# A separate 16-bit copy of the rows for the third pass of two projections

## The chip, the cores and the metric

One NeuronCore of a Trainium2 chip. The metric is the device time of one execution in microseconds (us); lower is better. All inputs, weights and the output are 32-bit floats in device memory.

## What is computed

One block of a decoder for 512 rows (tokens) of 2048 columns. The stages, in the reference's words cut to what matters:

```python
h = rms_norm(x, norm1_g[l])
z = h @ w_in[l]
...
o_rw = rwkv7_mix(...)            # 512 x 1024
o_att = swa_attention(...)       # 512 x 1024
p_rw = o_rw @ w_branch[l, :RW_DIM]
p_att = o_att @ w_branch[l, RW_DIM:]
x = x + (g_rw * p_rw + g_att * p_att) @ w_out[l]
...
u = h @ w_up                     # 2048 x 11264, h = rms_norm(x, norm2_g[l])
c = up[:, 0:S] * conv_w[0] + up[:, 1:S + 1] * conv_w[1] + up[:, 2:S + 2] * conv_w[2] + conv_b
val, gate = jnp.split(c, 2, axis=-1)
x = x + (silu(gate) * val) @ w_down
```

The change concerns two of the five projections: the branch projection (`w_branch`) and the up projection (`w_up`).

## The kernel before, in words

**Precision.** TensorE multiplies in a rounded 32-bit type (`F32R`) or in 16 bits (`BF16`). Every projection splits both operands into a high part in `F32R` and a low part in `BF16`: ScalarE (ACT) copies the 32-bit number into the high part, which rounds it, and VectorE (DVE) subtracts the high part from the number to get the low part. Each weight block of 128 x 128 is then multiplied in three passes which add into the same accumulator in PSUM:

1. high weights by high rows, both `F32R`;
2. the upper 16 bits of the high weights by low rows;
3. low weights by the upper 16 bits of the high rows.

The upper 16 bits are not stored apart. The helper `top` (lines 247 to 249) reads the high part as pairs of 16-bit numbers and takes every second one, so the operand's numbers lie four bytes apart. The weights are the stationary operand of a matmul, loaded first; the rows are the moving operand.

**Order of the stages.** Input projection with attention and the recurrence in between (up to about 1124 us of the profile), branch projection (1124 to 1298), output projection (to 1454), up projection (to 2316), down projection (to the end).

**Branch projection** (lines 980 to 1001). There are 16 strips of 128 output columns, and for each two parts: the recurrent rows `rhi`, `rlo` and the attention rows `ahi`, `alo`, eight blocks of 128 in each. `project` (line 273) goes through a part in groups of four weight blocks: `load_w` (line 255) loads 256 KB on the SyncE queue, splits it (ACT at L262, DVE at L263) into one of four buffers, and then the three passes follow, four matmuls of 512 columns each (L283). The rows are split ahead of the stage by `split` (L216, L217): the recurrent rows pinned in program order, two at a time with a gate's strip of the input projection between them, the attention rows left to the scheduler.

**Up projection** (class `Block`, lines 1150 on). Matrix multiplication in seven products instead of eight per column block, on halves of rows and columns. Rows are held as seven operands of 8 blocks x 256 columns, named `b11`, `b21`, `b22`, `t1`, `t2`, `t3`, `t4`; each has a high and a low tile in `bq`. There are 44 column blocks with seven products each, named `P1`, `P2`, `P7`, `P6`, `P5`, `Q4`, `P3`. A product takes one weight tile of 128 x 1024: `prep` splits it two steps ahead (ACT at L1177, DVE at L1179, three buffers), `run` issues its 24 matmuls of 256 columns (three passes of eight, L1196). The instructions of this stage are pinned to program order on each engine.

The row operands are made while the first products already run: `high` (L1142) is an ACT copy of 2048 columns, `low` (L1146) the DVE subtract. Between them stand DVE sums that make one operand from others (L1388, L1393, L1403, L1414), and the weight splits of `prep`. The calls are written out by hand; a cutting of it:

```python
prep(9)
pin(dve.scalar_tensor_tensor(q12, q11, -1.0, q22, op0=ALU.mult, op1=ALU.subtract))   # L1403
run(7)
...
high("t2", q12)
prep(10)
run(8)
low("t2", q12)
```

`run(8)` to `run(11)` are the products `P7` of the first four column blocks and use `t3`; `run(12)` is the first that uses `t2`.

**Memory.** Tiles are taken from pools that are stacked from the left or the right end of the memory; a tile that comes to lie on an earlier one waits for that one's last use. The two result tiles `u0`, `u1` of the up projection are cleared at their edge by GpSimd (POOL) at L1424.

Of the kernel before, what the change touches and what calls it, by code (L numbers as in the profile page):

```python
# [9 lines left out]
F32R = mybir.dt.float32r  # L10
F16 = mybir.dt.float16
BF16 = mybir.dt.bfloat16
I32 = mybir.dt.int32
AF = mybir.ActivationFunctionType
# [5 lines left out]
P = 128  # L20
S = 512
# [114 lines left out]
def block_kernel(ctx: ExitStack, tc: tile.TileContext, d: Dims, a: dict, out: bass.AP):  # L136
    nc = tc.nc
    act, dve, pool, pe, sync = nc.scalar, nc.vector, nc.gpsimd, nc.tensor, nc.sync
    NK, NP, NQ, NKV, NF = d.NK, d.NP, d.NQ, d.NKV, d.NF
# [29 lines left out]
    big1 = abc.enter_context(tc.tile_pool(name="big1", bufs=1))  # L169
# [40 lines left out]
    pin = tc.keep_in_program_order  # L210
# [4 lines left out]
    def split(hi, lo, src, pin=free):  # L215
        pin(act.activation(hi, src, AF.Copy))  # L216
        pin(dve.tensor_tensor(lo, src, hi.bitcast(F32) if hi.dtype == F32R else hi, op=ALU.subtract))  # L217
# [6 lines left out]
    for f in range(NPRE):  # L224
        w, t = a["w_up"][f], {n: up_d[f, n] for n in ("s3", "s1", "P6", "P3")}
# [21 lines left out]
    def top(x):  # L247
        x = x.bitcast(BF16)
        return x[(slice(None),) * (len(x.shape) - 1) + (slice(1, None, 2),)]
# [20 lines left out]
            sums_along()()  # L270
        return hi, lo

    def project(acc, src, xhi, xlo, pre=()):
        nk = src.shape[1]
        for k0 in range(0, nk, 4):
            n = min(4, nk - k0)
            whi, wlo = pre[k0 // 4] if k0 // 4 < len(pre) else load_w(src[:, k0 : k0 + n])
            ops = [[(whi[:, j], xhi[:, k0 + j]) for j in range(n)],
                   [(top(whi[:, j]), xlo[:, k0 + j]) for j in range(n)],
                   [(wlo[:, j], top(xhi[:, k0 + j])) for j in range(n)]]  # L280
            for i, part in enumerate(ops):
                for j, (l, r) in enumerate(part):
                    stream.append(pe.matmul(acc, l, r, start=k0 + i + j == 0, stop=k0 + n == nk and i == 2 and j == n - 1))  # L283
# [3 lines left out]
    def big(pl, nm, tag, dt=F32R):  # L287
        return pl.tile([P, BIG], dt, name=nm, tag=tag)

    def by_k(t, n=NK):  # L290
        return t[:, : n * S].rearrange("p (k s) -> p k s", s=S)
# [3 lines left out]
    if True:  # L295
        xhi = by_k(big(big1, "xhi", "h1"))
        xlo = by_k(big(big1, "xlo", "l1", BF16))
# [34 lines left out]

        def ztile(c0):
            acc = accp.tile([P, S], F32, name="acc", tag="acc")
            project(acc, zt[c0], xhi, xlo, first.pop(c0, ()))
            return acc

        acc_k = ztile(d.c_ka)
# [561 lines left out]
        xbs = ExitStack()  # L900
        xbp = xbs.enter_context(tc.tile_pool(name="xb", bufs=1, reuse_waits="tile"))
        tb = xbs.enter_context(tc.tile_pool(name="tb", bufs=4, reuse_waits="tile"))
        rhi, rlo = (xbp.tile([P, NP, S], t, name=f"r{e}") for e, t in (("hi", F32R), ("lo", BF16)))
        with tc.tile_pool(name="ain", bufs=1, side="right", reuse_waits="tile") as ainp:
            ain = [ainp.tile([P, NQ // 2, S], F32, name=f"ain{i}") for i in range(2)]
            rin = [ainp.tile([P, S], F32, name=f"rin{i}") for i in range(NP)]
            for i in range(NP):
                pool.dma_start(rin[i], o_rw_d[i])
            for i in range(2):
                pool.dma_start(ain[i], o_at_d.rearrange("(i n p) s -> i p n s", i=2, p=P)[i])  # L910
            wp["step"] = 4
            for i in range(4):
                emit_gate()

            for i in range(NP):
                split(rhi[:, i], rlo[:, i], rin[i], pin)
                if i % 2:
                    emit_gate()
            while gates:
                emit_gate()  # L920
            for ins, at in zip(entries, LAST):
                behind(ins, stream[base + at - 1])
            ahi = by_k(big(big1, "ahi", "h1"), NQ)
            alo = by_k(big(big1, "alo", "l1", BF16), NQ)
            for i in range(NQ):
                split(ahi[:, i], alo[:, i], ain[2 * i // NQ][:, i % (NQ // 2)])
    pa.close()


# [42 lines left out]
    with ExitStack() as pbb:  # L972
        accp = pbb.enter_context(tc.tile_pool(name="accB", bufs=4, space=PSUM, side="right", reuse_waits="tile"))
        mp = pbb.enter_context(tc.tile_pool(name="mt", bufs=2, side="right", reuse_waits="tile"))
        XC = NT * d.D // NK

        parts = ((rhi, rlo, 0, NP, 0), (ahi, alo, NP, NQ, 1))
        order = [(m + e, i) for m in range(0, NK - 4, 2) for i in (0, 1) for e in range(2)]
        order += [(m, i) for i in (1, 0) for m in range(NK - 4, NK)]
        g = {}  # L980
        for m, i in order:
            hi, lo, r0, n, gi = parts[i]
            second = m in g
            if not second:
                g[m] = tb.tile([P, 2, S], F32, name="gin", tag="gin")
                for j in range(2):
                    src = gate_d[(j * NK + m) * P : (j * NK + m + 1) * P]
                    if m < 4:
                        pin(sync.dma_start(g[m][:, j], src))
                    else:  # L990
                        act.dma_start(g[m][:, j], src)
            acc = accp.tile([P, S], F32, name="acc", tag="acc")
            project(acc, a["w_b"][m].rearrange("p (k c) -> p k c", c=P)[:, r0 : r0 + n], hi, lo)
            if second:
                w = min(XC, d.D)
                for e in range(m * XC, (m + 1) * XC, w):
                    t, c0 = divmod(e, d.D)
                    with tc.issue_after(wp["last"].ins):
                        sync.dma_start(x1(t, slice(c0, c0 + w)), xd[t * P : (t + 1) * P, c0 : c0 + w])
            gt = g[m][:, gi]  # L1000
            dve.scalar_tensor_tensor(gt, gt, 1.0, acc, op0=ALU.add, op1=ALU.mult)
            if second:

                dve.tensor_tensor(g[m][:, 0], g[m][:, 0], g[m][:, 1], op=ALU.add)
                if m % 2:
                    mt = [g[m + e][:, 0] for e in (-1, 0)]
                    tq = mp.tile([P, 4, TH], F32, name="tq", tag="tq")
                    factors(tq, *mt, 0)
                    factors(tq, *mt, 1)
                    store_factors(pool, "o", m // 2, *mt, tq)  # L1010
# [68 lines left out]

    upx = ExitStack()  # L1080
    bqp = upx.enter_context(tc.tile_pool(name="bqA", bufs=1, reuse_waits="tile"))
    bq = {n: [bqp.tile([P, KH, TH], t, name=f"{n}{i}") for i, t in enumerate((F32R, BF16))] for n in ("b11", "b21")}
    hp = hps.enter_context(tc.tile_pool(name="hhlO", bufs=3, reuse_waits="tile"))
    NCC = d.D // S
    ssp = tcp.tile([P, NT, NCC], F32, name="ssp")
# [52 lines left out]
    def halves(t):  # L1138
        return t.rearrange("p (a k) s -> p a (k s)", a=2)

    def high(n, q, pin=pin):
        pin(act.activation(halves(bq[n][0]), q, AF.Copy))  # L1142

    def low(n, q, pin=pin):
        hi, lo = (halves(x) for x in bq[n])
        pin(dve.tensor_tensor(lo, q, hi.bitcast(F32), op=ALU.subtract))  # L1146

    us = []
# [2 lines left out]
    class Block:  # L1151
# [29 lines left out]
        def mm(self, n):  # L1181
            if n == "P1":
                x = ups.tile([P, S], F32, name="X", tag="X")
                self.X = x[:, :TH]
                self.Z = x[:, TH:] if self.f < NPRE else upy.tile([P, S], F32, name="Z", tag="Y")[:, :TH]
            if n == "P7":
                self.Y = upy.tile([P, S], F32, name="Y", tag="Y")[:, :TH]
            into = {"P2": "Z", "P7": "Y", "Q4": "Y"}.get(n, "X")
            ps = getattr(self, "Z" if self.apart and n in ("P5", "P3") else into)
            start = n in ("P1", "P7") or n == "P2" and self.f >= NPRE or n == "P5" and self.apart  # L1190
            whi, wlo = (x.rearrange("p (k c) -> p k c", c=P) for x in self.hl.pop(n))
            xh, xl = bq[{"P1": "b11", "P2": "b21", "P7": "t3", "P6": "t2", "P5": "t1", "Q4": "t4", "P3": "b22"}[n]]
            for i in range(3):
                for k in range(KH):
                    l, r = ((whi[:, k], xh[:, k]), (top(whi[:, k]), xl[:, k]), (wlo[:, k], top(xh[:, k])))[i]
                    pin(pe.matmul(ps, l, r, start=start and k + i == 0, stop=k == KH - 1 and i == 2, skip_group_check=True))  # L1196

        def out(self, n):
# [141 lines left out]
    with tc.tile_pool(name="sqp", bufs=1, side="right", reuse_waits="tile") as sqp:  # L1340
# [3 lines left out]
        for i in range(len(PRODUCTS)):  # L1344
# [14 lines left out]
            if last:  # L1359
# [8 lines left out]


    bqp = upx.enter_context(tc.tile_pool(name="bqB", bufs=1, reuse_waits="tile"))  # L1370
    bq.update({n: [bqp.tile([P, KH, TH], t, name=f"{n}{i}") for i, t in enumerate((F32R, BF16))]
               for n in ("b22", "t1", "t3", "t2", "t4")})
    up = upx.enter_context(tc.tile_pool(name="upw", bufs=1, side="left", reuse_waits="tile"))

# [182 lines left out]
```

## Time and profile before

| | |
|---|---|
| median of 3 runs | 2743.89 us (2741.99 to 2744.76) |
| the profiled execution | 2743.16 us |
| its span, first to last instruction | 2741.3 us |
| granted TensorE clock, mean | 0.999 |
| branch projection, L283, matmuls of 512 columns | 1124 to 1298 us |
| up projection, L1196, matmuls of 256 columns | 1454 to 2316 us |

How to read the lines below. PE is TensorE's matmuls, PEld its weight loads, DVE VectorE, ACT ScalarE, POOL GpSimd, SP SyncE. A row of a group names line, engine, operation, output and inputs by the program's names (buffer numbers left out), the shape and the count; behind the bar stand the busy time of the group in us, the mean duration of one in ns, and the idle time before them with what ended it. A row of the timeline gives the start, the duration of the run of equal instructions, and in brackets the idle time before. Matmuls are pipelined: one lasts longer than the distance to the start of the next, and the busy time of a group counts overlapping time once. A few matmul records are missing from the trace. A row of waits gives who waited for whom, the time in all, how often, and the longest.

### The profile page before, as it was taken

What the parts mean: (1) busy time and instruction counts of PE and PEld (TensorE: products, weight loads), DVE (VectorE), ACT (ScalarE), POOL (GpSimd) and SP (SyncE); (2) the same over time, 40 slices, a digit from 0 to 9 for tenths busy, and PEclk for the clock granted to TensorE, in tenths of its full rate; (3) what the DMA queues carried; (4) which work ended last, traced back from release to release, by engine and by line L of the source; (5) the groups of instructions that cost most, each with busy time, mean ns of one, the idle gap of its engine ahead of it and who ended that gap; (6) DMA issues with size and microseconds to landing.
All of it is one profiled execution on the core that took longest, in us unless ns stands there. A gap on an engine that the chain in (4) does not pass through costs nothing.

```text
span 2741.3 us, 45720 instructions
## 1 busy us (share of the span) xinstructions
PE 2685.9 (98%) x17227; PEld 1832.6 (67%) x17410; DVE 1995.1 (73%) x3476; ACT 1334.9 (49%) x2245; POOL 231.3 (8%) x308
## 2 busy tenths in 40 slices
PE   8999999999999999999999999999999999999999
PEld 4555566566566665555558889999999998555554
DVE  6787777777887775445668788888888888555655
ACT  5455445534544543322466555555555555444443
POOL 0001011111111001011000111111111110000000
PEclk9999999999999999999999999999999999999999
DMA  6557788778878767888785889898898889877775
GB/s 237 156 152 203 203 215 217 207 193 228 213 186 221 187 180 188 269 249 283 253 281 166 229 238 250 250 241 235 243 251 244 236 239 278 299 241 245 258 257 180
DMA packets 228333, 623.80 MB, mean 228 GB/s; under 512 B 24960, under 2 KB 45072, under 8 KB 227088
## 3 DMA queue, kind: packets, MB, share of 16 engines
q1 hardware_dynamic: 159552, 445.23, 49.3%
q0 software_dynamic: 37216, 136.33, 25.7%
q10 hardware_dynamic: 31344, 39.31, 4.1%
q8 instruction: 136, 2.23, 0.3%
q14 instruction: 85, 0.70, 0.1%
HBM read 571.16 MB, written 191.18 MB: 278 GB/s over the span
## 4 chain that ended last, share of the span: by engine, by line
PE 83%; DVE 8%; DMA 4%; ACT 2%; issue 2%; SPq 0%; DVEq 0%; ACTq 0%
PE acc L283 27%; PE X L1196 16%; PE X L1061 11%; PE Y L1061 9%; PE Y L1196 8%; PE Z L1196 4%; DMA raw<-in_w_z_dram 1%; DVE wlo L263 1%; PE psS L829 1%; PE psG L820 1%; PE bulk L757 1%; DMA rsb<-rsd 1%; PE bulk L805 1%; DVE wlo L1179 1%; PE psU L823 1%
## 5 line engine op out<-in xcount | busy, mean ns | idle before, releaser
L1053 DVE TENSOR_TENSOR wlo<-raw,whi 128x1024 bf16<-128x1024 f32 x210 | 256.7, 1225 | 192.5 <-ACT whi L1052 192.4
L283 PE MATMUL acc<-xhi,whi 128*128 128x512 f32 x1152 | 377.9, 441 | 10.7 <-ACT whi L262 10.3
L262 ACT ACTIVATE whi<-raw 128x512 fp32r<-128x512 f32 x352 | 220.0, 627 | 327.2 <-PE acc L283 269.6
L1052 ACT ACTIVATE whi<-raw 128x1024 fp32r<-128x1024 f32 x210 | 221.7, 1057 | 278.6 <-PE X L1061 146.0
L283 PE MATMUL acc<-xhi,wlo 128*128 128x512 bf16 x1107 | 311.8, 388 | 2.6
L263 DVE TENSOR_TENSOR wlo<-raw,whi 128x512 bf16<-128x512 f32 x352 | 240.0, 688 | 102.0 <-ACT whi L262 67.3
L283 PE MATMUL acc<-xlo,whi 128*128 128x512 bf16 x1080 | 302.1, 384 | 4.0 <-issue 0.5
L1179 DVE TENSOR_TENSOR wlo<-raw,whi 128x1024 bf16<-128x1024 f32 x184 | 224.8, 1223 | 72.3 <-ACT whi L1177 71.6
L1196 PEld LDWEIGHTS <-wlo 128*128 128x128 bf16 x2464 | 237.4, 96 | 39.5
L283 PEld LDWEIGHTS acc<-xhi,whi 128*128 128x128 f32 x1152 | 210.8, 189 | 69.3 <-ACT whi L262 11.3
L1196 PEld LDWEIGHTS <-whi 128*128 128x128 bf16 x2464 | 216.9, 98 | 34.7
L1177 ACT ACTIVATE whi<-a 128x1024 fp32r<-128x1024 f32 x124 | 130.8, 1055 | 223.0 <-DVE a L1172 208.5
L283 PEld LDWEIGHTS <-wlo 128*128 128x128 bf16 x1408 | 134.5, 98 | 155.6 <-issue 5.3
L283 PEld LDWEIGHTS <-whi 128*128 128x128 bf16 x1408 | 112.1, 100 | 158.8 <-issue 94.3
L1179 DVE TENSOR_TENSOR wlo<-a,whi 128x1024 bf16<-128x1024 f32 x124 | 152.0, 1225 | 63.8 <-ACT whi L1177 62.6
L1177 ACT ACTIVATE whi<-raw 128x1024 fp32r<-128x1024 f32 x184 | 192.1, 1045 | 3.3 <-PE X L1196 1.6
L1196 PE MATMUL X<-b,whi 128*128 128x256 f32 (+1 forms) x1472 | 192.1, 283 | 0.7 <-ACT whi L1177 0.3
L1196 PE MATMUL X<-t,whi 128*128 128x256 f32 (+1 forms) x1408 | 183.8, 283 | 2.9 <-ACT u L1223 2.5
L1196 PE MATMUL Y<-t,whi 128*128 128x256 f32 (+1 forms) x1408 | 183.8, 283 | 0.4 <-DVE u L1225 0.4
L1061 PE MATMUL X<-whi,hhi 128*128 128x512 f32 x480 | 153.3, 441 | 1.4 <-ACT whi L1052 1.4
L1061 PEld LDWEIGHTS <-hhi 128*128 128x128 bf16 x840 | 81.5, 97 | 103.7
L1247 DVE SCALAR_TENSOR_TENSOR c<-u,par,c 128x512 f32<-128x512 f32 x176 | 131.5, 747 | 14.2 <-ACT c L1244 14.0
(387 smaller groups left out, 4551.6 us busy)
## 6 DMA issues: line engine op xcount, KB each, us to landing
raw<-in_w_up_dram SPq DMA_DIRECT2D x170, 512.0 KB
raw<-in_w_z_dram SPq DMA_DIRECT2D x288, 256.0 KB
s_dn<-in_w_dn_dram POOLq DMA_DIRECT2D x88, 512.0 KB, 7.2
raw<-s_dn SPq DMA_DIRECT2D x88, 512.0 KB
raw<-in_w_up_dram POOLq DMA_DIRECT2D x80, 512.0 KB, 8.7
raw<-in_w_dn_dram SPq DMA_DIRECT2D x66, 512.0 KB
s_dn<-in_w_dn_dram SPq DMA_DIRECT2D x44, 512.0 KB
s_dn<-s_dn SPq DMA_DIRECT2D x44, 512.0 KB
```

What stands on the lines that cost most here:

```text
L262: act.activation(hi, raw, AF.Copy)
L263: dve.tensor_tensor(lo, raw, hi.bitcast(F32), op=ALU.subtract)
L283: stream.append(pe.matmul(acc, l, r, start=k0 + i + j == 0, stop=k0 + n == nk and i == 2 and j == n - 1))
L757: ins = pe.matmul(ps[:, n], wt[:, 0, n], both(n), start=True, stop=False)
L805: pin(pe.transpose(ps[:, e, q], X[:, e, 2 * q : 2 * q + 2].rearrange("p n c -> p (n c)"), id16))
L1052: act.activation(whi, wr, AF.Copy)
L1053: dve.tensor_tensor(wlo, wr, whi.bitcast(F32), op=ALU.subtract)
L1061: pe.matmul(dst, l, r, start=fst and j == 0, stop=lst and j == 2, skip_group_check=True)
L1177: pin(act.activation(hi, t, AF.Copy))
L1179: return lambda: pin(dve.tensor_tensor(lo, t, hi.bitcast(F32), op=ALU.subtract))
L1196: pin(pe.matmul(ps, l, r, start=start and k + i == 0, stop=k == KH - 1 and i == 2, skip_group_check=True))
L1247: pin(dve.scalar_tensor_tensor(t, u[:, i, j + 1 : j + 1 + S], cw[:, j + 1, ci : ci + 1], t, op0=ALU.mult, op1=ALU.add))
```

## The change

A third tile, `BF16` and contiguous, is kept for each row operand of the two projections. ACT fills it with one more copy from the same 32-bit source, so it holds the rows rounded to 16 bits, where `top` took the upper half of the high part. The third pass reads this tile in place of `top(...)`. The input projection, which also goes through `project`, keeps `top`, and so do the output and down projections, and every second pass for its weights.

```diff
-    def project(acc, src, xhi, xlo, pre=()):
+    def project(acc, src, xhi, xlo, x16=None, pre=()):
...
-                   [(wlo[:, j], top(xhi[:, k0 + j])) for j in range(n)]]
+                   [(wlo[:, j], x16[:, k0 + j] if x16 is not None else top(xhi[:, k0 + j])) for j in range(n)]]
...
-        rhi, rlo = (xbp.tile([P, NP, S], t, name=f"r{e}") for e, t in (("hi", F32R), ("lo", BF16)))
+        rhi, rlo, r16 = (xbp.tile([P, NP, S], t, name=f"r{e}") for e, t in (("hi", F32R), ("lo", BF16), ("16", BF16)))
...
                 split(rhi[:, i], rlo[:, i], rin[i], pin)
+                pin(act.activation(r16[:, i], rin[i], AF.Copy))
...
-            alo = by_k(big(big1, "alo", "l1", BF16), NQ)
+            al = big1.tile([P, 2 * NQ * S], BF16, name="alo", tag="l1")
+            alo, a16 = (al[:, e * NQ * S : (e + 1) * NQ * S].rearrange("p (k s) -> p k s", s=S) for e in range(2))
             for i in range(NQ):
                 split(ahi[:, i], alo[:, i], ain[2 * i // NQ][:, i % (NQ // 2)])
+                act.activation(a16[:, i], ain[2 * i // NQ][:, i % (NQ // 2)], AF.Copy)
...
-            project(acc, a["w_b"][m].rearrange("p (k c) -> p k c", c=P)[:, r0 : r0 + n], hi, lo)
+            project(acc, a["w_b"][m].rearrange("p (k c) -> p k c", c=P)[:, r0 : r0 + n], hi, lo, h16)
...
     def high(n, q, pin=pin):
         pin(act.activation(halves(bq[n][0]), q, AF.Copy))
+        pin(act.activation(halves(bq[n][2]), q, AF.Copy))
...
-                    l, r = ((whi[:, k], xh[:, k]), (top(whi[:, k]), xl[:, k]), (wlo[:, k], top(xh[:, k])))[i]
+                    l, r = ((whi[:, k], xh[:, k]), (top(whi[:, k]), xl[:, k]), (wlo[:, k], xb[:, k]))[i]
```

The tiles of `bq` are made in two pools, `bqA` for `b11` and `b21` and `bqB` for the other five; both get a third `BF16` tile of 4 KB a partition for each operand. `r16` takes 8 KB a partition behind `rlo`; `a16` takes the unused half of the tile that holds `alo`.

More of the change, by code (lines that the diff above doesn't have):

```diff
@@ L334, in ztile @@
             acc = accp.tile([P, S], F32, name="acc", tag="acc")
-            project(acc, zt[c0], xhi, xlo, first.pop(c0, ()))
+            project(acc, zt[c0], xhi, xlo, pre=first.pop(c0, ()))
             return acc
@@ L975, in block_kernel @@
         XC = NT * d.D // NK
-        parts = ((rhi, rlo, 0, NP, 0), (ahi, alo, NP, NQ, 1))
+        parts = ((rhi, rlo, r16, 0, NP, 0), (ahi, alo, a16, NP, NQ, 1))
         order = [(m + e, i) for m in range(0, NK - 4, 2) for i in (0, 1) for e in range(2)]
@@ L981, in block_kernel @@
         for m, i in order:
-            hi, lo, r0, n, gi = parts[i]
+            hi, lo, h16, r0, n, gi = parts[i]
             second = m in g
@@ L1081, in block_kernel @@
     bqp = upx.enter_context(tc.tile_pool(name="bqA", bufs=1, reuse_waits="tile"))
-    bq = {n: [bqp.tile([P, KH, TH], t, name=f"{n}{i}") for i, t in enumerate((F32R, BF16))] for n in ("b11", "b21")}
+    bq = {n: [bqp.tile([P, KH, TH], t, name=f"{n}{i}") for i, t in enumerate((F32R, BF16, BF16))] for n in ("b11", "b21")}
     hp = hps.enter_context(tc.tile_pool(name="hhlO", bufs=3, reuse_waits="tile"))
@@ L1142, in high @@
         pin(act.activation(halves(bq[n][0]), q, AF.Copy))
+        pin(act.activation(halves(bq[n][2]), q, AF.Copy))
     def low(n, q, pin=pin):
-        hi, lo = (halves(x) for x in bq[n])
+        hi, lo = (halves(x) for x in bq[n][:2])
         pin(dve.tensor_tensor(lo, q, hi.bitcast(F32), op=ALU.subtract))
@@ L1191, in mm @@
             whi, wlo = (x.rearrange("p (k c) -> p k c", c=P) for x in self.hl.pop(n))
-            xh, xl = bq[{"P1": "b11", "P2": "b21", "P7": "t3", "P6": "t2", "P5": "t1", "Q4": "t4", "P3": "b22"}[n]]
+            xh, xl, xb = bq[{"P1": "b11", "P2": "b21", "P7": "t3", "P6": "t2", "P5": "t1", "Q4": "t4", "P3": "b22"}[n]]
             for i in range(3):
                 for k in range(KH):
-                    l, r = ((whi[:, k], xh[:, k]), (top(whi[:, k]), xl[:, k]), (wlo[:, k], top(xh[:, k])))[i]
+                    l, r = ((whi[:, k], xh[:, k]), (top(whi[:, k]), xl[:, k]), (wlo[:, k], xb[:, k]))[i]
                     pin(pe.matmul(ps, l, r, start=start and k + i == 0, stop=k == KH - 1 and i == 2, skip_group_check=True))
@@ L1370, in block_kernel @@
     bqp = upx.enter_context(tc.tile_pool(name="bqB", bufs=1, reuse_waits="tile"))
-    bq.update({n: [bqp.tile([P, KH, TH], t, name=f"{n}{i}") for i, t in enumerate((F32R, BF16))]
+    bq.update({n: [bqp.tile([P, KH, TH], t, name=f"{n}{i}") for i, t in enumerate((F32R, BF16, BF16))]
                for n in ("b22", "t1", "t3", "t2", "t4")})
```

## The prediction

> **What bounds the kernel now.** I read the page's first lines and its chain of waits, then a table of stretches, then the groups of matmuls with shapes kept apart, then narrow pieces of the timeline.
>
> ```profile
> span 2741.3 us, 45720 instructions
> PE 2685.9 (98%) x17227; PEld 1832.6 (67%) x17410; DVE 1995.1 (73%) x3476; ACT 1334.9 (49%) x2245; POOL 231.3 (8%) x308
> PE 83%; DVE 8%; DMA 4%; ACT 2%; issue 2%; SPq 0%; DVEq 0%; ACTq 0%
> PE acc L283 27%; PE X L1196 16%; PE X L1061 11%; PE Y L1061 9%; PE Y L1196 8%; PE Z L1196 4%; DMA raw<-in_w_z_dram 1%; DVE wlo L263 1%; PE psS L829 1%; PE psG L820 1%; PE bulk L757 1%; DMA rsb<-rsd 1%; PE bulk L805 1%; DVE wlo L1179 1%; PE psU L823 1%
> ```
>
> TensorE is busy 98% of the span and carries 83% of the chain. The lines edited are two of its heaviest, L283 and L1196. By stretch (branch projection; start of the up projection; its steady part):
>
> ```profile
> core 0: us, PE busy (x) PEld busy (x) DVE busy (x) ACT busy (x) POOL busy (x), PEclk, DMA share, GB/s
> 1124.00:1298.00 174.00, 173.07 (x757) 93.29 (x771) 90.67 (x151) 47.11 (x77) 19.56 (x27) 1.00 0.82 259
> 1454.00:1550.00 96.00, 93.50 (x812) 84.75 (x813) 81.04 (x100) 60.03 (x82) 5.21 (x6) 1.00 0.71 215
> 1750.00:1950.00 200.00, 200.00 (x1750) 181.24 (x1749) 164.27 (x199) 105.32 (x146) 21.55 (x25) 1.00 0.89 241
> ```
>
> TensorE has no gap in the steady part, next to none in the branch stretch, and its clock is full. So the time of both stages is the number of matmuls times the distance between their starts, and the question is whether that distance depends on how the moving operand lies in memory.
>
> **The distance between starts.** Each weight block goes through three passes: full high weights by high rows, upper halves of the weights by low rows, low weights by upper halves of the rows. The last is the one changed: its moving operand is 16-bit numbers four bytes apart; in the second pass they lie side by side. Both passes, 256 wide (L1196), as groups and as six matmuls each of the timeline:
>
> ```profile
> L1196 PE MATMUL X<-b,wlo 128*128 128x256 bf16 x736 | 98.6, 275 | 0.0
> L1196 PE MATMUL X<-b,whi 128*128 128x256 bf16 x736 | 96.6, 274 | 0.0
> 1902.41 0.82 PE L1196 MATMUL Z<-b,whi 128*128 128x256 bf16 x6
> 1903.30 0.84 PE L1196 MATMUL Z<-b,wlo 128*128 128x256 bf16 x6
> ```
>
> A row of n pipelined matmuls lasts n-1 distances and one duration. The 736 strided ones are 92 passes of eight: 98.6/92 = 1.072 us, less 0.275, over 7 = 113.8 ns. The contiguous ones give 110.9 ns the same way, but their first distance still follows 32-bit weights; the six inside the pass give (0.82-0.274)/5 = 109.2 ns, against 113.0 for the strided six. I take 113.8 to 109.2, 4.6 ns; the bound below is 113.8-110.9 = 2.9 ns.
>
> At 512 wide, the branch's strided pass and, in the output projection, a pass with contiguous moving operand and one with strided:
>
> ```profile
> 1294.21 1.07 PE L283 MATMUL acc<-rhi,wlo 128*128 128x512 bf16 x4
> L283 PE MATMUL acc<-rhi,wlo 128*128 128x512 bf16 x124 | 33.2, 387 | 0.3
> 1302.40 1.02 PE L1061 MATMUL X<-wlo,hhi 128*128 128x512 bf16 x4
> L1061 PE MATMUL X<-wlo,hhi 128*128 128x512 bf16 x466 | 121.0, 378 | 0.4
> 1301.48 1.08 PE L1061 MATMUL X<-whi,hlo 128*128 128x512 bf16 x4
> L1061 PE MATMUL X<-whi,hlo 128*128 128x512 bf16 x465 | 126.7, 390 | 1.1
> ```
>
> (1.07-0.387)/3 = 228 ns and (1.08-0.390)/3 = 230 strided, (1.02-0.378)/3 = 214 contiguous: some 14 ns, though rounding alone moves each by 3. Twice the 256-wide difference is 9.2 ns. I take 10.5, nearer that one since its rows are sharper.
>
> In all these rows a strided moving operand meets contiguous weights, and a contiguous one strided weights. Is the stride at fault, or the contiguous weights? One group has both contiguous, in 16 bits and 128 wide, eight in a row:
>
> ```profile
> L805 PE MATMUL bulk<-id,XIW 128*128 128x128 f16 x256 | 19.8, 220 | 3.7 <-DVE XIW L801 1.9
> ```
>
> 19.8/32 = 619 ns a row, less 220, over 7 = 57 ns: contiguous weights can change every 57 ns, so they aren't what holds a matmul at 114. I put it on the stride.
>
> A rule of the Trainium skill speaks against that. Its page Advanced Engine Details and Errata, section SBUF Cachelines, says that memory is read in 16-byte lines, that further accesses to a line already hit run at full rate, two hits a line being enough, and that the stride tolerated goes by type. Four bytes apart puts four numbers on a line, so by the rule this stride is free and the edit gains nothing. The rows above, 113.8 against 109.2 and 228 against 214, don't agree.
>
> **What the change takes away.** Up: 44 column blocks x 7 products x 8 = 2464 matmuls x 4.6 ns = 11.3 us (7.1 at 2.9 ns). Branch: 16 strips x 2 parts x 8 = 256 x 10.5 ns = 2.7 us (2.4 to 3.5). Together 14.0. A slower pass isn't expected: the rows have no contiguous pass slower than its strided partner.
>
> **What it adds** is ScalarE copies: 7 of 2048 columns in `high`, 8 of `r16`, 8 of `a16`. VectorE and the DMA queues get nothing. No copy with 16-bit output from 32-bit rows at these sizes is in the trace; I price them as the 32-bit ones beside them. The start of the up projection first:
>
> ```profile
> 1474.91 1.91 ACT L1142 ACTIVATE t<-x 128x2048 fp32r<-128x2048 f32 x1
> 1476.72 1.04 ACT L1177 ACTIVATE whi<-raw 128x1024 fp32r<-128x1024 f32 x1
> 1477.80 1.23 DVE L1179 TENSOR_TENSOR wlo<-raw,whi 128x1024 bf16<-128x1024 f32 x1 [0.94 <-ACT whi L1177]
> 1479.18 0.42 DVE L1209 TENSOR_TENSOR t<-t,X 128x256 f32<-128x256 f32 x1 [0.15 <-PE X L1196]
> 1484.32 2.29 DVE L1403 SCALAR_TENSOR_TENSOR x<-x,x 128x2048 f32<-128x2048 f32 x1
> 1486.64 1.92 ACT L1142 ACTIVATE t<-x 128x2048 fp32r<-128x2048 f32 x1 [4.56 <-DVE x L1403]
> 1488.46 1.99 ACT L1177 ACTIVATE whi<-raw 128x1024 fp32r<-128x1024 f32 x2
> 1489.88 2.09 PE L1196 MATMUL Y<-t,whi 128*128 128x256 f32 x16
> ```
>
> One copy holds ScalarE 1476.72-1474.91 = 1.81 us, and program order there is pinned, so the next weight split stands behind it. For `t3`, the split at 1476.72 slips to 1478.5 and its VectorE subtract from 1477.80 to 1479.6. VectorE then has work without a gap over 0.15 us up to the end of L1403 (1484.32+2.29 = 1486.6), which slips to about 1488.1. That releases `high("t2")`: 1488.2 instead of 1486.64. Two copies of 1.82 and the split, done 1.05 after its start, give 1492.9 for the weights that TensorE begins on at 1489.88: a stall of 3.0 us. The first ten products had won 0.4 us by then, which it swallows. It is 1.5 if only the copy of `t2` counts, and nothing if the copies slip into gaps. The other five copies I price at nothing: ScalarE's idle time hides them (96-60 us in that stretch), and followed in the same way the later splits come ahead of their products, by margins under 1 us in places. Without that cover they cost 1.8 each.
>
> The branch:
>
> ```profile
> 1126.71 3.74 ACT L216 ACTIVATE ahi<-ain 128x512 fp32r<-128x512 f32 x7
> 1130.36 1.13 ACT L262 ACTIVATE whi<-raw 128x512 fp32r<-128x512 f32 x2
> 1135.09 1.28 PE L283 MATMUL acc<-ahi,whi 128*128 128x512 f32 x4
> ```
>
> Copies of 512 follow each other at (1130.36-1126.71)/7 = 0.52 us. Two of `r16` and eight of `a16` fall ahead of the split at 1130.36: 5.2 us, so the first of it is done at 1136.2, while TensorE wants it at 1135.09: 1.1 us late. Nothing if the scheduler, free to move `a16`, puts some of them behind. The other six `r16` copies stand where four weight buffers are ahead: nothing.
>
> Memory: the copies take 8 KB, then 28 KB a partition, and shift later tiles. By the sizes in the code `u1` comes to lie over `x01`, and its clearing must wait for the last reader of that tile:
>
> ```profile
> 1069.67 0.15 POOL L1424 MEMSET u<- 128x4 f32 x2 [10.83 <-DVE yc L839]
> 1495.15 2.29 DVE L1414 SCALAR_TENSOR_TENSOR x<-x,x 128x2048 f32<-128x2048 f32 x1
> 1508.39 0.89 POOL L1165 DMA_DIRECT2D raw<-in_w_up_dram  x1 [77.59 <-DMA raw<-P_u]
> ```
>
> It runs at 1069.67 now and would run some 1500. What queues behind it on POOL is the transfer of 1508.39, so it costs nothing unless L1414 slips by over 10 us.
>
> Sum: 14.0 - 3.0 - 0.4 - 1.1 = 9.5 us off. The profiled execution took 2743.16 us (span 2741.3 and 1.9 around it), 0.7 under the median of the runs, 2743.89. From the first: 2733.7; from the median, which I give: 2734.4.
>
> **Rivals.** (1) *No faster pass.* The stride is free, or something else holds the third pass at 114 ns. Against it: two shapes and two stages where slow goes with strided. For it: no row shows this very pass contiguous, with contiguous weights. Only the stalls stay, 4.1 us: 2748.0. The cacheline rule above is the page's form of it. Chance 0.06.
>
> (2) *Another limit takes over in the steady up projection.* DMA engines are at 0.89 there and VectorE at 164 of 200 us. If transfers held the pace, only the branch would gain: 2743.9 - 2.7 + 4.1 = 2745.3. Against it, SyncE's queue over the 700 us from 1600:
>
> ```profile
> SPq L1163 <- DVE wlo L1179: 374.7, 60, 9.6
> ```
>
> The loads wait for buffers to come free, not the buffers for loads. Chance 0.04.
>
> (3) *Slower: ScalarE becomes the bound at the two starts.* If each copy pushes the weight split behind it and TensorE has no cover, all of 7 x 1.81 + 16 x 0.52 = 21.0 us is paid: 2743.9 - 14.0 + 21.0 = 2750.9. It decides above 19.5 us of stalls; 14.0 makes it even. For it: stalls follow from pinned order. Against: ScalarE is idle 36 of 96 us there and 127 of 174 in the branch. Chance 0.05.
>
> **Numbers.** My forecast has 0.85. A measurement tells about 0.2%, 5.5 us, from no change. The forecast's best is 11.3+3.5 = 14.8 without stalls: 2729; its worst 7.1+2.4 less stalls of 6.5: 2741. Of its 0.85, 0.03 lies within 0.2%, and some 0.04 outside the range. So faster 0.82, same 0.03+0.06+0.04 = 0.13, slower 0.05; range 2729 to 2741.
>
> **What would show it.** The group `X<-b,wlo` should come to (7 x 109.2 + 274) x 92 = 95.5 us; the steady product, now 200 us for 1750/24 = 72.9 of them or 2.74 us, to about 2.71; the branch's third pass from 1.07 to 1.02 us. TensorE should show new waits on `whi` near 1490 and 1135, and ScalarE 21 us more. A third pass still at 1.07 us for eight proves me wrong at the root; waits on `whi` well over 4 us in all prove the costs wrong; the rates right and the steady product unmoved would be rival 2.

## The result, and the profile after

The changed kernel takes 2751.16 us (median of 8 runs, 2747.72 to 2752.71); the kernel before, run beside it on the same chip, 2742.98 (8 runs, 2733.94 to 2747.5). The ratio is 1.0029 with an interval of 1.0017 to 1.0040: slower by 8.2 us, where 9.5 us less was forecast. The profiled execution took 2752.39 us, 9.2 more than that of before. Lines are numbered by the changed kernel from here on: L1196 has become L1200, L1177 L1181, L1223 L1227.

The page of the changed kernel, its first lines (busy time, share, instructions):

```profile
span 2750.6 us, 45749 instructions
PE 2681.5 (97%) x17227; PEld 1837.7 (67%) x17410; DVE 1995.5 (73%) x3476; ACT 1356.4 (49%) x2268; POOL 232.2 (8%) x308
```

TensorE is busy 4.4 us less than before in a span 9.3 us longer, so it idles 13.7 us more; ScalarE works 21.5 us more, in 23 more instructions. The groups of the changed kernel, shapes kept apart: the third pass of the up projection, then the new copies (a group's busy time, mean ns of one, idle time before):

```profile
L1200 PE MATMUL X<-b,wlo 128*128 128x256 bf16 x736 | 95.4, 273 | 0.0
L1146 ACT ACTIVATE t<-x 128x2048 bf16<-128x2048 f32 x4 | 7.6, 1897 | 0.0
L917 ACT ACTIVATE r<-rin 128x512 bf16<-128x512 f32 x8 | 4.9, 617 | 0.0
```

This group of the third pass fell from 98.6 to 95.4 us. The matmuls are quicker as forecast; the time went into waits around them. The three stretches of before, in the same table (PE busy is the first number after the stretch's length):

```profile
core 0: us, PE busy (x) PEld busy (x) DVE busy (x) ACT busy (x) POOL busy (x), PEclk, DMA share, GB/s
1124.00:1298.00 174.00, 170.44 (x754) 93.23 (x768) 91.37 (x151) 51.53 (x86) 19.62 (x27) 1.00 0.81 254
...
1454.00:1550.00 96.00, 89.14 (x759) 80.18 (x758) 75.80 (x92) 65.95 (x81) 3.59 (x5) 0.98 0.65 197
...
1750.00:1950.00 200.00, 199.14 (x1755) 182.40 (x1753) 162.51 (x197) 106.10 (x147) 23.36 (x27) 1.00 0.90 245
```

TensorE idles 3.6 us in the branch stretch (0.9 before), 6.9 us at the start of the up projection (2.5 before), where the mean clock is also 0.98, and 0.9 us even in the steady part, where it had no gap. By stage, each measured between the starts of the same weight loads in both traces (the start of the up projection is 1470.6 to 1567.1 in the trace of before, the steady pairs are 1653.9 to 2307.8):

| stage | before | after | difference |
|---|---|---|---|
| up to the branch projection | | | -0.7 |
| branch projection | 174.27 | 174.95 | +0.7 |
| output projection | 156.43 | 158.20 | +1.8 |
| up projection, its start | 96.50 | 103.60 | +7.1 |
| the next piece | | | +0.5 |
| 17 steady pairs of column blocks | 653.90 | 650.67 | -3.2 |
| end of the up projection | | | +0.9 |
| down projection | 418.62 | 420.81 | +2.2 |

**The branch's start.** ScalarE of the changed kernel, timeline (start, duration, operation, idle time before in brackets); L929 makes `a16`, shown under `alo`, the tile in which it lies:

```profile
1123.07 1.15 ACT L929 ACTIVATE alo<-ain 128x512 bf16<-128x512 f32 x2 [2.08 <-PE acc L283]
1124.13 0.58 ACT L378 ACTIVATE gt<-acc 128x512 f32<-128x512 f32 x1
...
1133.45 0.62 ACT L929 ACTIVATE alo<-ain 128x512 bf16<-128x512 f32 x1
1133.97 2.19 ACT L262 ACTIVATE whi<-raw 128x512 fp32r<-128x512 f32 x4
```

TensorE of the changed kernel there:

```profile
1130.92 1.03 PE L283 MATMUL acc<-r,wlo 128*128 128x512 bf16 x4
1134.65 1.19 PE L283 MATMUL acc<-rhi,whi 128*128 128x512 f32 x4 [2.70 <-ACT whi L262]
```

At this place the kernel before split a weight block (in its own trace `1123.75 0.63 ACT L262 ACTIVATE whi<-raw 128x512 fp32r<-128x512 f32 x1 [2.08 <-PE acc L283]`). In the changed one the scheduler put two `a16` copies there, which read only rows loaded well before, and the split came at 1133.97, behind the last of the sixteen new copies. TensorE waited 2.70 us for it. The pass itself, four matmuls, takes 1.03 us as against 1.07.

**The up projection's start.** Timeline of ScalarE in the changed kernel; L1145 makes the high operand, L1146 is the new copy, L1181 the weight split:

```profile
1478.43 1.90 ACT L1146 ACTIVATE t<-x 128x2048 bf16<-128x2048 f32 x1
...
1489.91 1.92 ACT L1145 ACTIVATE t<-x 128x2048 fp32r<-128x2048 f32 x1 [6.19 <-DVE x L1407]
1491.73 1.90 ACT L1146 ACTIVATE t<-x 128x2048 bf16<-128x2048 f32 x1
1493.53 1.99 ACT L1181 ACTIVATE whi<-raw 128x1024 fp32r<-128x1024 f32 x2
```

and of TensorE:

```profile
1494.62 3.24 PE L1200 MATMUL Y<-t,whi 128*128 128x256 f32 x16 [2.98 <-ACT whi L1181]
1497.65 1.59 PE L1200 MATMUL Y<-t,wlo 128*128 128x256 bf16 x8
...
1520.51 2.10 PE L1200 MATMUL Y<-t,whi 128*128 128x256 f32 x16 [2.28 <-DVE u L1229]
```

The forecast stall is there at its size, 2.98 us. But the sixteen matmuls after it last 3.24 us, where the sixteen at 1520.51 last 2.10; the table of stretches for the changed kernel says why (the number behind POOL's count is the granted clock):

```profile
1495.50:1498.70 3.20, 3.20 (x16) 2.33 (x16) 3.20 (x3) 3.20 (x4) 0.00 (x0) 0.50 0.49 160
```

The granted clock was half for 3.4 us (1495.4 to 1498.8), which cost another 1.7. And 26 us later there is a second stall, 2.28 us on a VectorE sum. VectorE of the changed kernel:

```profile
1517.84 2.29 DVE L1150 TENSOR_TENSOR b<-x,b 128x2048 bf16<-128x2048 f32 x1
1520.04 0.42 DVE L1229 TENSOR_TENSOR u<-u,Y 128x256 f32<-128x256 f32 x1
```

The sum that frees an accumulator (L1229) stood in pinned order behind the subtract of `b22` (L1150), which the copies ahead had delayed. The stage holds a second piece of half clock, from 1563.6 on, behind a gap of 2.55 us; the kernel before has that gap too (2.52 us) and no drop behind it.

**The steady part.** A pair of column blocks, 14 products, took 38.453 us before (in the median). In the changed kernel pairs take from 37.99 to 38.92, 38.18 in the median. TensorE of the changed kernel at the place where it waits in most pairs:

```profile
1661.46 1.04 PE L1200 MATMUL Z<-b,wlo 128*128 128x256 bf16 x8
1663.32 1.45 PE L1200 MATMUL X<-t,whi 128*128 128x256 f32 x10 [0.82 <-ACT u L1227]
```

and ScalarE of the same kernel and pair (ACTq rows are DMA issues on ScalarE's own queue):

```profile
1655.52 1.58 ACTq L969 DMA_DIRECT2D h_dn<-c  x1
1656.06 0.37 ACT L1227 ACTIVATE u<-X 128x256 f32<-128x256 f32 x1
1657.19 0.46 ACTq L970 DMA_DIRECT2D h_dn<-tq  x1
1657.70 0.81 ACT L1248 ACTIVATE c<-u,par 128x512 f32<-128x512 f32 x1 [1.27 <-DVE wlo L1183]
...
1661.42 0.63 ACT L1254 ACTIVATE c<-c 128x512 f32<-128x512 f32 x1 [1.95 <-DVE c L1251]
1661.95 1.04 ACT L1181 ACTIVATE whi<-raw 128x1024 fp32r<-128x1024 f32 x1
1662.90 0.36 ACT L1227 ACTIVATE u<-X 128x256 f32<-128x256 f32 x1
```

Read it backwards. The matmul at 1663.32 overwrites the accumulator that the copy L1227 reads until 1663.26. That copy stands behind a split and the activation L1254, which ends a convolution begun by L1248 at 1657.70. L1248 is put down to VectorE, but began 0.05 us after the issue of L970 ended (1657.19 + 0.46 = 1657.65): it stood behind three issues of `h_dn` stores. Among the 17 pairs the two with the longest issue in the middle, 1.51 and 1.41 us, are the longest, 38.92 and 38.86 us. The kernel before at one such place, ScalarE and then TensorE's matmul:

```profile
1724.61 0.81 ACT L1244 ACTIVATE c<-u,par 128x512 f32<-128x512 f32 x1 [0.26 <-issue]
...
1728.33 0.63 ACT L1250 ACTIVATE c<-c 128x512 f32<-128x512 f32 x1 [1.96 <-DVE c L1247]
1728.87 1.04 ACT L1177 ACTIVATE whi<-raw 128x1024 fp32r<-128x1024 f32 x1
1729.82 0.36 ACT L1223 ACTIVATE u<-X 128x256 f32<-128x256 f32 x1
...
1730.85 1.32 PE L1196 MATMUL X<-t,whi 128*128 128x256 f32 x9
```

There the copy ended at 1730.18, and TensorE's matmul came at 1730.85. Over the pairs of before, the copy was ahead by 0.05 to 0.87 us. A pair that is to be 0.47 us shorter uses most of that up.

### The profile page after: what moved, and what is told of

Same layout as the page of the kernel before. It is cut to its first block, busy times and chain, and to the rows that moved or that the text cites. A ratio compares the mean times of both kernels' runs of the same rounds, so it can differ in the third digit from the quotient of the medians.

```text
span 2750.6 us, 45749 instructions
## 1 busy us (share of the span) xinstructions
PE 2681.5 (97%) x17227; PEld 1837.7 (67%) x17410; DVE 1995.5 (73%) x3476; ACT 1356.4 (49%) x2268; POOL 232.2 (8%) x308
## 5 line engine op out<-in xcount | busy, mean ns | idle before, releaser
L283 PE MATMUL acc<-xhi,whi 128*128 128x512 f32 x1152 | 377.5, 441 | 11.2 <-ACT whi L262 10.8
L262 ACT ACTIVATE whi<-raw 128x512 fp32r<-128x512 f32 x352 | 219.8, 629 | 314.4 <-PE acc L283 234.6
L283 PE MATMUL acc<-xhi,wlo 128*128 128x512 bf16 x1107 | 312.5, 389 | 2.6
L283 PE MATMUL acc<-xlo,whi 128*128 128x512 bf16 x1080 | 301.8, 383 | 4.2 <-issue 0.7
L1200 PEld LDWEIGHTS <-wlo 128*128 128x128 bf16 x2464 | 241.5, 98 | 28.3
L283 PEld LDWEIGHTS acc<-xhi,whi 128*128 128x128 f32 x1152 | 210.6, 189 | 70.1 <-ACT whi L262 12.2
L1181 ACT ACTIVATE whi<-a 128x1024 fp32r<-128x1024 f32 x124 | 130.9, 1055 | 241.0 <-DVE a L1176 239.6
L1200 PEld LDWEIGHTS <-whi 128*128 128x128 bf16 x2464 | 217.6, 99 | 35.4
L283 PEld LDWEIGHTS <-wlo 128*128 128x128 bf16 x1408 | 135.0, 98 | 154.4 <-issue 6.0
L283 PEld LDWEIGHTS <-whi 128*128 128x128 bf16 x1408 | 111.9, 100 | 159.3 <-issue 95.2
L1181 ACT ACTIVATE whi<-raw 128x1024 fp32r<-128x1024 f32 x184 | 192.2, 1047 | 3.6 <-PE Y L1200 3.0
L1200 PE MATMUL X<-b,whi 128*128 128x256 f32 (+1 forms) x1472 | 191.8, 283 | 0.5 <-DVE u L1221 0.3
L1200 PE MATMUL Y<-t,whi 128*128 128x256 f32 (+1 forms) x1408 | 184.7, 284 | 7.0 <-DVE u L1229 4.0
L1200 PE MATMUL X<-t,whi 128*128 128x256 f32 (+1 forms) x1408 | 185.4, 285 | 5.5 <-ACT u L1227 5.4
```

Source lines behind the costliest of these rows:

```text
L262: act.activation(hi, raw, AF.Copy)
L1181: pin(act.activation(hi, t, AF.Copy))
```

## The experiments

Ratios are against the kernel before on the same chip, with 95% intervals; medians are of 5 to 10 runs, of 10 to 29 for before.

**copies_only**: all copies made, the third passes reading the upper halves as before.

```diff
-                   [(wlo[:, j], x16[:, k0 + j] if x16 is not None else top(xhi[:, k0 + j])) for j in range(n)]]
+                   [(wlo[:, j], top(xhi[:, k0 + j])) for j in range(n)]]
...
-                    l, r = ((whi[:, k], xh[:, k]), (top(whi[:, k]), xl[:, k]), (wlo[:, k], xb[:, k]))[i]
+                    l, r = ((whi[:, k], xh[:, k]), (top(whi[:, k]), xl[:, k]), (wlo[:, k], top(xh[:, k])))[i]
```

> All three 16-bit tiles are made as in the changed kernel, but the third pass reads the upper halves of the high parts as before: the cost of the copies without the faster pass. Theory A (the loss has two sources: copies that stand ahead of weight splits at the starts of the branch and of the up projection, and a ScalarE/VectorE chain in the steady up projection that takes back over half of the gain there): 8 to 13 us slower than before, with TensorE waits on whi near 1131 (about 2.7 us) and 1492 (about 3 us), and the steady pair of column blocks at 38.45 us as before. Rival B (the pass gains its full 14 us and the copies cost all the rest): 20 to 24 us slower than before. Rival C (the loss is chance of the clock): within 5 us of before.

2755.44 us, ratio 1.0043 (1.0025 to 1.0060): 12.9 us slower than before (2742.56). The three longest of its waits of TensorE from 1440 to 1600 us (time in all, times, longest):

```profile
PE Y L1200 <- ACT whi L1181: 2.8, 1, 2.8
PE X L1200 <- ACT u L1227: 2.5, 1, 2.5
PE Y L1200 <- DVE u L1229: 2.1, 1, 2.1
```

The first and third are new; the second, near 1566, is in the kernel before too. The start of the up projection took 105.47 us (96.50 before), the branch 177.10 (174.27), a steady pair 38.453 as before. So in the trace the copies cost 2.8 + 9.0 = 11.8 at the two starts, and nothing in the steady part. Three pieces of half clock, from 1495.4, 1522.7 and 1567.1 on, are some 5 us of the 11.8.

**rate_only**: no copy; the third pass reads the low tile of the rows, which is contiguous too. So low by low is computed where low by high stood.

```diff
+            project(acc, a["w_b"][m].rearrange("p (k c) -> p k c", c=P)[:, r0 : r0 + n], hi, lo, lo)
...
-                    l, r = (..., (wlo[:, k], top(xh[:, k])))[i]
+                    l, r = (..., (wlo[:, k], xl[:, k]))[i]
```

> No 16-bit copies and no tiles for them: the third pass of the branch and up projections reads the low tiles of the rows, which are contiguous, in place of the upper halves (so it adds low by low in place of low by high). The faster pass alone. Theory A: 6 to 9 us faster than before: the third pass at 109 ns and 215 ns between starts, but in the steady up projection TensorE waits once per two column blocks for ScalarE's copy of an accumulator, so that a pair takes 38.0 to 38.2 us where 14 products of the new rate would take 37.9, more when a store's issue on ScalarE is long. Rival B: 13 to 14 us faster, no such waits. Rival C: within 5 us of the changed kernel less its stalls, no clear figure.

2733.22 us, ratio 0.9967 (0.9950 to 0.9985): 9.3 us off, not 14. Its group of the third pass is the changed kernel's:

```profile
L1196 PE MATMUL X<-b,wlo 128*128 128x256 bf16 x736 | 95.4, 273 | 0.0
```

Branch 172.33 us; pairs 37.98 to 38.50, median 38.125. No copies, and yet pairs are uneven.

**rate_late** and **before_late**: the same kernel, and the kernel before, with the three stores issued two steps later in the block, behind the activation that ends the convolution.

```diff
-            if part == 0 and f and f % 2 == 0:
+            if part == 2 and f and f % 2 == 0:
                 B[f - 1].keep()
```

> As rate_only, and the three stores of a finished pair of column blocks are issued on ScalarE's queue two steps later, ahead of the third convolution step in place of the first, so behind the accumulator copy that TensorE waits for. Theory A with these issues as the tight link: 11 to 14 us faster than before, pairs at 37.9 to 38.0 us. Theory A with another tight link (VectorE's order): as rate_only, 6 to 9 us faster. Rival B: as rate_only, 13 to 14 us faster.

> The kernel before with only the later stores: the control. Theory A: the same as before within 2 us, since the accumulator copy is early enough there in nearly all pairs (0.05 to 0.85 us). If it is faster by over 4 us, the stores cost something that the trace of before doesn't show as a wait of TensorE.

rate_late: 2729.74 us, ratio 0.9955 (0.9935 to 0.9976), 12.8 off. before_late: 2741.12, ratio 0.9994 (0.9984 to 1.0005), no difference. Of the 17 steady pairs of rate_late 15 take 37.986 or 37.987 us, and of those of before_late 15 take 38.453 or 38.454. ScalarE of rate_late, the place shown above:

```profile
1717.46 0.37 ACT L1223 ACTIVATE u<-X 128x256 f32<-128x256 f32 x1
1717.72 0.80 ACT L1244 ACTIVATE c<-u,par 128x512 f32<-128x512 f32 x1
...
1721.43 0.63 ACT L1250 ACTIVATE c<-c 128x512 f32<-128x512 f32 x1 [1.96 <-DVE c L1247]
...
1722.92 0.36 ACT L1223 ACTIVATE u<-X 128x256 f32<-128x256 f32 x1
```

The convolution starts 0.26 us after the copy before it; in the changed kernel that is 1657.70 - 1656.06 = 1.64, and from there to the activation both take 3.7 us. The second copy ends at 1723.28, and TensorE's matmul starts at 1724.10 without a wait. The same edit is worth nothing where TensorE is slower, and 3.5 us by the medians where it is faster (2733.22 to 2729.74; those two intervals overlap; in the traces the 17 pairs fell from 648.18 to 646.25): the issues were hidden before, by a margin that the faster matmuls took away.

**after_late**: the changed kernel with the same late stores. **branch_only**: the change in the branch projection alone.

> The changed kernel with only the stores late; the copies stay ahead of the weight splits. Theory A: 3 to 6 us less than the changed kernel (8.2 slower than before), so 2 to 5 us slower than before: pairs at 37.99 us, the stalls at the two starts as in the changed kernel. If the stalls are what matters alone, it stays 8 us slower.

> The change in the branch projection alone (r16 and a16 and the third pass there), the up projection as before. Theory A: the third pass gains 2.7 us, the late weight split near 1131 costs 2.7 to 3.1 and the output projection starts up to 1.9 later: 0 to 3 us slower than before. If the branch part is not among the sources of the loss: 2 to 3 us faster.

after_late: 2743.11, ratio 1.0002 (0.9990 to 1.0015), beside 2741.34 for before: 1.8 slower by the medians, which is not clear of noise, and just under what was expected. Of its 17 pairs 15 are back at 37.987, and what is left of the loss is at the starts. branch_only: 2744.47, ratio 1.0018 (1.0005 to 1.0031), 3.1 slower, at the edge of what was expected. TensorE's waits in its branch stretch:

```profile
PE acc L283 <- ACT whi L262: 2.7, 1, 2.7
```

Branch 174.96 us against 174.27: the quicker pass wins back some 2 of a stall of 2.7.

**placed** and **placed_late**: the whole change, with the copies moved to where ScalarE has time, those of `r16` excepted. The moved copies read the high operand instead of the source; `a16` is made behind the first two splits for the first attention part, those of the up projection behind the next weight split (that of `b11` right behind its high operand). placed_late also issues the stores late.

```diff
+            if (m, i) == (0, 1):
+                pre = [load_w(wsrc[:, k : k + 4]) for k in range(0, n, 4)]
+                for k in range(n):
+                    act.activation(a16[:, k], ahi[:, k].bitcast(F32), AF.Copy)
...
+    def copy16(n, pin=pin):
+        pin(act.activation(halves(bq[n][2]), halves(bq[n][0]).bitcast(F32), AF.Copy))
...
     prep(9)
+    copy16("t3")
...
     prep(12)
+    copy16("t2")
```

> The copies moved as in placed_late, the stores where they were. Theory A: 6 to 10 us faster than before, as rate_only was (9.3), pairs between 38.0 and 38.5 us. Rival B: within 5 us of before or slower.

> The change whole, with its copies moved and the stores late. a16 is copied from the high part behind the first two weight splits of the attention part; each copy of the up projection is taken from the high part and stands behind the next weight splits instead of ahead of them; r16 stays; the stores of a pair as in rate_late. Theory A (copies ahead of weight splits, and the stores ahead of the accumulator copy, are what the changed kernel loses by): 9 to 13 us faster than before, pairs at 37.99 us, no TensorE wait over 1.5 us on whi near 1131 and 1490, and no drop of the clock near 1495. Rival B (ScalarE's 21 us of copies cost wherever they stand): at least 5 us slower than rate_late, so not over 8 us faster than before.

placed: 2735.85, ratio 0.9980 (0.9970 to 0.9990), 5.5 off, just under what was expected; its pairs take 37.99 to 38.92 us, where 38.5 was expected at most. placed_late: 2730.3, ratio 0.9963 (0.9948 to 0.9977), 11.0 off. ScalarE of placed_late, the two starts:

```profile
1128.12 1.14 ACT L262 ACTIVATE whi<-raw 128x512 fp32r<-128x512 f32 x2
1129.16 4.26 ACT L1000 ACTIVATE alo<-ahi 128x512 bf16<-128x512 f32 x8
1133.33 1.13 ACT L262 ACTIVATE whi<-raw 128x512 fp32r<-128x512 f32 x2
```

```profile
1483.07 1.92 ACT L1150 ACTIVATE t<-x 128x2048 fp32r<-128x2048 f32 x1 [2.76 <-DVE x L1417]
1484.90 1.99 ACT L1188 ACTIVATE whi<-raw 128x1024 fp32r<-128x1024 f32 x2
```

Splits now go ahead of the copies, and the splits that came at 1493.53 come at 1484.90. The branch takes 171.99 us, the start of the up projection 96.92, a pair 37.987. The matmuls are those of the changed kernel, and the copies are as many and as large. Against its own runs of before each, the changed kernel is 8.2 us slower and this one 11.0 faster: 19.2 us go by where the copies and the stores stand. It is the fastest version here that computes the whole of it, with pool_late beside it.

**pool_late**: all the 16-bit copies on GpSimd instead (shown for the up projection), and late stores.

```diff
-        pin(act.activation(halves(bq[n][2]), q, AF.Copy))
+        pin(pool.tensor_copy(halves(bq[n][2]), q))
```

> The changed kernel with all its 16-bit copies on GpSimd in place of ScalarE, at the same places in program order, and the stores late. Theory A (only work ahead of the weight splits on ScalarE costs): 9 to 13 us faster than before, as placed_late (0.9963), if GpSimd has a copy of 2048 columns done within the 10 us or so up to its first use. A rival: GpSimd is slow at it, or slows VectorE beside it, and the third pass of the first products waits for the copies: not over 5 us faster, with TensorE waits on GpSimd or longer VectorE operations between 1454 and 1520.

2731.87 us, ratio 0.9961 (0.9947 to 0.9975), 10.6 off. Its copies as a group:

```profile
L1146 POOL CAST t<-x 128x2048 bf16<-128x2048 f32 x4 | 9.8, 2456 | 33.4 <-DVE x L1397 23.2 <-DVE x L1407 10.2
```

2.46 us in the mean as against 1.90 on ScalarE (three of these four took 1.89 and one 4.15; times on GpSimd are rough), and TensorE waits for one of the copies once, 0.9 us. That is as good as placed_late, with no copy moved in the program: the price of the copies was their queue.

## Why the prediction was wrong

The forecast of the faster pass held; three steps about what the copies and the speed-up run into did not: the price of the copies in the branch, the five copies at nothing, and the steady part without another limit.

**The gain per matmul was right.** The group came to 95.4 us for a forecast of 95.5, the branch pass to 1.03 for 1.02, and rate_late, whose steady part hardly waits, gained 12.8 for 14.0 (in its trace 2.1 in the branch and 9.3 in the up projection; the rest lies in stages that the edit leaves alone). A pair fell by 38.453 - 37.987 = 0.466 us over 112 third-pass matmuls, 4.2 ns each, for a forecast of 4.6. Rival 1 falls: contiguous rows beside contiguous weights are quicker. The rule that the prediction draws from the Trainium skill (page "Advanced Engine Details and Errata", section "SBUF Cachelines"), by which the stride is free, does not describe this operand.

**"TensorE wants it at 1135.09: 1.1 us late" failed.** The prediction put the eight free copies behind the splits that the trace already showed at 1123.75 and before. The scheduler put two of them ahead of one that ran at 1123.75, and that split became the late one. The stall was 2.70 us; with it the branch lost 0.7 us where 2.7 - 1.1 = 1.6 was to be gained. The gain of 2.7 us was too large as well: rate_only and placed_late show 1.9 and 2.3 (174.27 less 172.33 and 171.99).

**The stall of 3.0 us at `t2` was right, "the other five copies I price at nothing" was not.** A second stall of 2.28 us followed the copies of `t4` and `b22`, on a VectorE sum behind a delayed subtract. The prediction had seen margins under 1 us there and still gave them no price. Nor did it price what a stall does to the clock: 1.7 us after the first, and 1.7 more from 1563.6 on. Together the start of the up projection lost 7.1 us, where 3.0 less 1.2 for its 33 faster products was forecast: 5.3 on top. The runs bear the clock out: the mean granted clock was 0.9966 over the 8 runs of the changed kernel and 0.9981 over the 57 of before in the experiments, by which some 4 of the 8.2 us are half clock (an estimate, 0.0015 x 2745).

**The sentence on the steady part failed, and cost as much**: "the time of both stages is the number of matmuls times the distance between their starts". No gap in TensorE's row was read as no other limit near. Rival 2 names another limit in the steady part, but asked only for transfers. The next limit was a ScalarE copy once per 14 products, 0.05 to 0.87 us ahead. Of 17 x 0.466 = 7.9 us (8.8 at the 4.6 ns of the forecast) the steady part kept 3.2, 5.6 short of the forecast. That the store issues set it is shown by the pairs of rate_late and after_late, 37.987 us long in 15 of 17, and by before_late, where the same edit moves nothing.

Rival 3 came near in sign and time (2750.9), and the time is luck, for its mechanism is half of it: the starts lost some 12 us in copies_only, not 21, a part of that to the clock, and the steady part had to lose gain as well.

**What stays open.** The 1.8 us of the output projection are one late start behind a transfer (1.5 us without a matmul). The stage is longer by 1.2 to 2.3 us in the traces of all five kernels with late stores too, before_late among them, and not in those of copies_only, rate_only, placed and branch_only, so it doesn't go with the change; why it comes is not known. The down projection's 2.2 us hold one piece of half clock (1.7). The costs of copies_only (+12.9) and rate_only (-9.3) add up to 3.6, less than the 8.2 measured; each has an interval of some 5 us either way. By the traces the difference lies in the steady part (rate_only kept 5.7 us there, the changed kernel 3.2; the middle issue of a pair took 0.69 us in the mean in the one and 0.79 in the other), in the output projection and in the down projection. Why that issue's length varies is not known.

## What to carry to other kernels

Where an engine shows no gap, ask how late its next supplier could come before it would show one, and price a speed-up only up to that slack: here 0.47 us per pair met 0.05 to 0.87. A copy that is added to an engine with half its time idle is still paid where it stands ahead of a split that something waits for, so place new work behind the splits, pinned, instead of where its source becomes ready. The issues of three stores held up ScalarE's queue, so DMA issues are to stand behind the work that others wait for.

## What the runs showed of the hardware

**The moving operand's stride.** 16-bit rows four bytes apart cost some 4% per matmul: 113.8 ns from start to start at 256 wide before, and (95.4/92 us - 0.273)/7 = 109.1 ns in the changed kernel.

**Half clock after short gaps.** Four times in the changed kernel's trace the granted clock fell to 0.50 for 3.41 us, three of them after gaps of 2.98, 2.55 and 1.94 us of TensorE; the 2.55 is in the trace of before as 2.52, and no drop follows there. Over the eleven traces of this case, with the first 45 us and the end left out, a drop followed 1 of 36 gaps of 1.2 to 1.8 us, 7 of 16 from 1.8 to 2.2, 6 of 17 from 2.2 to 2.6, and 4 of 8 above. Each costs about 1.7 us on top of the gap. The Trainium skill (page "TensorE: Matmul & The Clock Gate", section "Why this matters for your kernels") advises against idle gaps of TensorE over some 3 us; the traces agree in the kind of harm and differ in the length, since 1.9 us sufficed. The traces also show which gap is followed by a drop. Within each trace the drops start whole multiples of 3.413 us apart (427, 20 and 229 of them in the changed kernel's). Divide the traces at these times into pieces of 3.413 us: all 15 pieces in which TensorE was idle for 2.0 us or more were followed by a drop, 3 of 20 with 1.5 to 2.0 us, and none with less. So a gap that lies across two pieces can pass without a drop, and whether a stall costs 1.7 us more depends on where it falls.

**Issues on ScalarE's queue.** The three stores that ScalarE issues per pair took 0.34, 1.58 and 0.46 us in the pair shown, and the middle one 0.48 to 1.51 over the 17 steady pairs of the changed kernel; compute behind them waited.
